# Experts with 4 KB weight rows, tokens fetched as rows by indirect DMA, results kept as rows in memory

## The chip, the cores and the metric

The kernel runs on one core of a Trainium2 chip. The metric is the device time of one execution in microseconds (us). Three runs of the kernel before gave 1471.57, 1472.33 and 1472.89 us, a median of 1472.33. The engines are PE (TensorE, matrix products), ACT (ScalarE), DVE (VectorE), POOL (GpSimd) and SP (SyncE, which only issues the weight loads here). PE reads its operands from SBUF, the on-chip memory, and writes to PSUM, which has eight banks of 512 float32 columns; ACT and DVE read PSUM, POOL does not.

## The reference

Two layers act on 256 tokens of 1024 values. Layer 0 is a mixer (sparse attention beside a gated delta rule) and a dense SwiGLU; layer 1 is a pooling mixer and a mixture of experts. Only the last stage is touched:

```python
def moe_ffn(x, router_w, wg, wu, wd):
    logits = jnp.einsum('bsd,de->bse', x, router_w).astype(F32)
    probs = jax.nn.softmax(logits, -1)
    top_p, top_i = lax.top_k(probs, TOP_K)                # 2 of 8
    top_p = top_p / jnp.sum(top_p, -1, keepdims=True)
    gate = jnp.sum(jax.nn.one_hot(top_i, N_EXPERTS) * top_p[..., None], axis=-2)
    y = jnp.zeros(x.shape, F32)
    for e in range(N_EXPERTS):
        y = y + gate[..., e:e + 1] * swiglu(x, wg[e], wu[e], wd[e])
    return y
```

`swiglu(x, wg, wu, wd)` is `(silu(x wg) * (x wu)) wd`, with wg and wu of 1024 x 3584 and wd of 3584 x 1024, all float32. A layer norm of `alpha * x + y` follows, which is the kernel's output. The eight experts hold 352 MB of weights, all of which are read.

## The kernel before, in words

The experts are worked through one after the other. Each computes on a buffer of C = 96 token slots; where an expert has more tokens than that, a loop behind a branch at the end does the rest (`tc.If(most > C)`).

Weights arrive in loads of 1 MB (`wchunk`, line 151) that SP issues into 16 staging buffers (`stg`), used in turn. Each load is worked on in two halves of 128 x 1024. ACT rounds a half into a high part `wh` (line 180), DVE subtracts it from the original for the low part `wl` (line 183), and there are four buffers of each. PE multiplies three times for each product (`mm3`, lines 187 to 189): low activations by high weights, high by low, high by high. For the gate weights of the first block of expert 0 the subtraction is given to POOL (`first`), and the rounding waits for `after`, a column of ones made from the routing.

An expert's 3584 hidden columns are seven blocks of 512. `up_block(b)` loads two 1 MB pieces of gate weights and two of up weights, each as rows of 512 columns (2 KB), accumulates them in two PSUM banks (`accg`, `accu`), then `swiglu_block` (lines 866 to 874) applies silu on ACT, multiplies on DVE, turns the 96 x 512 result with four PE transposes (`htp`) and splits it into a high and a low part in `hbc`. `down_block(b)` multiplies that with two 1 MB pieces of down weights (rows of 4 KB) into two banks `dacc`, held for the whole expert. Block b's `down_block` is written behind block b + 1's `up_block`.

Tokens enter and leave by PE. `gather(e)` (line 1059) makes a one-hot matrix `oh` of tokens by slots on DVE, multiplies the 256 x 1024 tokens `xt` by it on PE (16 matmuls of float32, which the trace shows as 32, into `gb`), splits the result into `ehl` (high and low), and transposes `oh` (`ohT`, copied to `ot`). It is issued ahead, in the previous expert's last block. At an expert's end `dacc` is split, PE multiplies it by `ot` (8 matmuls `scat`, lines 1125 and 1126), and DVE adds the result, times the gate, to `yt` (line 1128), which starts as `alpha * xt` (line 1150).

The order within each engine is set at build time by a scheduler that works with priorities and its own estimate of times; `wchunk`'s two halves have a high priority, and blocks under `urgent` a higher one.

Of the kernel before, what the change touches and what calls it, by code (L numbers as in the profile page):

```python
# [12 lines left out]
F32 = mybir.dt.float32  # L13
F32R = mybir.dt.float32r
# [94 lines left out]
def hybrid_kernel(ctx, tc, consts, bands, x, ev_w_in, ev_cmp_pe_k, ev_cmp_w_k, ev_cmp_pe_v, ev_cmp_w_v, ev_conv_w,  # L109
# [737 lines left out]
    def m_tile(i, name, dt=F32):  # L847
        return mp.tile([P, STG], dt, name=name, tag="m%d" % i)
# [196 lines left out]
    eh, el = (r3(ehl[:, o:o + KT * C], C) for o in (0, HALF))  # L1045
    hbc = r3(m_tile(2, "hbc", F32R), 512)
    turn = [0]

    def hpair():
        turn[0] ^= 2  # L1050
        return (hbc[:, turn[0] + i] for i in range(2))

    def bc(ap):
        return ap[:, :, None].to_broadcast(e3)
# [1 line left out]
    iota = cst("iota")  # L1056


    def gather(e):
        oh = late.tile([P, TT, C], F32, name="oh", tag="oh")  # L1060
        for t in range(TT):
            V.tensor_scalar(oh[:, t, :], iota[:, :C], rank[:, t, e:e + 1], sel[:, t, e:e + 1], op0=OP.is_equal, op1=OP.mult)
        for half in range(2):
# [7 lines left out]
        tp = bank("ohT", ps_tp)  # L1071
        for t in range(TT):
            T.transpose(tp[:C, t * P:(t + 1) * P], oh[:, t, :], ident)
        ot = late.tile([P, S], F32R, name="ot", tag="ot", bufs=2)[:C]
        A.copy(out=ot, in_=tp[:C, :S])
        return ot

    def expert(wg, wu, wd, gathered, gcol, ahead=None, after=None):
        ot = gathered
        dacc = [bank("dacc")[:C] for _ in range(2)]  # L1080
        nblk = DFE // 512
        def up_block(b):
            f0 = b * 512
            ac = {}
            for nm, wsrc in (("g", wg), ("u", wu)):
                ac[nm] = bank("acc" + nm)[:C]
# [6 lines left out]
            hb, hc = (r3(v[:, :4 * C], C) for v in hpair())  # L1093
            swiglu_block(ac["g"], ac["u"], 512, hb, hc, C)
            return hb, hc

        def down_block(b, hb, hc):
            last = b == nblk - 1
            loads = [wd[:, 4 * b + 2 * c:4 * b + 2 * c + 2, :] for c in range(2)]
            wcs = [wchunk([(src, D)], D) for src in loads] if last else None  # L1100
            for nbs in ([0], [1]) if last else ([0, 1],):
                for c in range(2):
                    wc = wcs[c] if last else wchunk([(loads[c], D)], D)
                    for k in range(2):
                        for nb in nbs:
                            mm3(dacc[nb], hb[:, 2 * c + k, :], hc[:, 2 * c + k, :], wc[k][0][:, nb * 512:(nb + 1) * 512],
                                wc[k][1][:, nb * 512:(nb + 1) * 512], b == 0 and c == 0 and k == 0,
                                last and c == 1 and k == 1)

        prev = up_block(0)  # L1110
        nxt = None
        for b in range(1, nblk):
            cur = up_block(b)
            if b == nblk - 1 and ahead is not None:
                nxt = gather(ahead)
            down_block(b - 1, *prev)
            prev = cur
        down_block(nblk - 1, *prev)
        ys_ = []
# [10 lines left out]
        return nxt  # L1130

    eg, eu, ed = od_exp_wg[0], od_exp_wu[0], od_exp_wd[0]
    sums = late.tile([P, TT, 2], F32, name="sums")
    with urgent(FIRST):
        got = gather(0)
# [10 lines left out]
    V.tensor_tensor(out=gate, in0=gate, in1=bc(m0), op=OP.mult)  # L1146
    nmax = late.tile([P, 1], I32, name="nmax")
    V.tensor_reduce(out=nmax, in_=rk[:, 16:24], axis=AX.X, op=OP.max)
    for t in range(TT):
        A.activation(yt[:, t, :], xt[:, t, :], AF.Copy, scale=late1[:, 1:2])  # L1150
    for e in range(NE):
        got = expert(krows(eg[e]), krows(eu[e]), krows(ed[e]), got, gate[:, :, e], e + 1 if e + 1 < NE else None,
                     after if e == 0 else None)

    g4, b4 = load_pair(od_ln2_g[0], od_ln2_b[0], stage_c[0].tile([P, STG], F32, name="g4b4", tag="stg"))

# [2 lines left out]
    with tc.If(most > C):  # L1159
        ring.clear()  # L1160
        stages[:] = [(stage_a, 4)]
        with tc.For_i(0, ROUNDS - 1, 1):
            V.tensor_scalar(rank, rank, -float(C), None, op0=OP.add)
            with tc.For_i(0, NE, 1) as i:
                def sub(w):
                    return w[bass.ds(i, 1)].rearrange("o (k p) n -> p (o k) n", p=P)

                expert(sub(eg), sub(eu), sub(ed), gather(0), gate[:, :, 0])
# [46 lines left out]
```

## Time and profile before

| | |
|---|---|
| median of three runs | 1472.33 us |
| profiled execution | 1473.03 us |
| its span, first to last instruction | 1471.2 us |
| PE busy | 1427.8 us (97%) |
| DVE busy | 1184.3 us (80%) |
| ACT busy | 976.8 us (66%) |
| DMA, mean over the span | 283 GB/s |

The experts begin with the first gather at 450.3 us and end about 15 us before the span does. The page's "busy" of PE overlaps from one matmul to the next: a 512-column matmul is listed with 0.39 us, yet the next starts about 0.23 us later. So starts are compared below, not durations. Each row of the timeline gives start, length, engine, line, operation, what it writes and reads, and how many instructions are merged; brackets give idle time before it and who ended it.

### The profile page before, as it was taken

What the parts mean: (1) busy time and instruction counts of PE and PEld (TensorE: products, weight loads), DVE (VectorE), ACT (ScalarE), POOL (GpSimd) and SP (SyncE); (2) the same over time, 40 slices, a digit from 0 to 9 for tenths busy, and PEclk for the clock granted to TensorE, in tenths of its full rate; (3) what the DMA queues carried; (4) which work ended last, traced back from release to release, by engine and by line L of the source; (5) the groups of instructions that cost most, each with busy time, mean ns of one, the idle gap of its engine ahead of it and who ended that gap; (6) DMA issues with size and microseconds to landing.
All of it is one profiled execution on the core that took longest, in us unless ns stands there. A gap on an engine that the chain in (4) does not pass through costs nothing. (4 is left out here: it accounts for less than half of the span.)

```text
span 1471.2 us, 18925 instructions
## 1 busy us (share of the span) xinstructions
PE 1427.8 (97%) x7006; PEld 1061.2 (72%) x7006; DVE 1184.3 (80%) x1524; ACT 976.8 (66%) x1216; POOL 20.0 (1%) x12
## 2 busy tenths in 40 slices
PE   8999988999998999999999999999999999999995
PEld 7898567888786777777777777777777777777663
DVE  6876655555567998999899899899989989989886
ACT  5745543444427777777777777777777777777773
POOL 0000020000002000000000000000000000000000
PEclk9999998999998999999999999999999999999998
DMA  8432039554864998999899899999989989999921
GB/s 294 141 104 101 1 101 330 183 189 158 307 223 166 378 373 323 362 371 370 314 372 373 312 372 371 343 344 371 370 312 375 372 321 364 367 347 335 353 113 60
DMA packets 188628, 416.89 MB, mean 283 GB/s; under 512 B 14104, under 2 KB 24816, under 8 KB 188528
## 3 DMA queue, kind: packets, MB, share of 16 engines
q1 hardware_dynamic: 188528, 415.61, 78.6%
q8 instruction: 57, 0.93, 0.3%
q14 instruction: 43, 0.35, 0.1%
HBM read 414.53 MB, written 1.05 MB: 282 GB/s over the span
## 5 line engine op out<-in xcount | busy, mean ns | idle before, releaser
L183 DVE TENSOR_TENSOR wl<-stg,wh 128x1024 fp32r<-128x1024 f32 (+1 forms) x765 | 914.3, 1221 | 181.9 <-ACT wh L180 174.5
L180 ACT CAST wh<-stg 128x1024 fp32r<-128x1024 f32 (+1 forms) x769 | 799.3, 1049 | 289.0 <-PE accg L189 81.7
L187 PE MATMUL accg<-wh,ehl 128*96 128x512 f32 x448 | 178.8, 399 | 1.9 <-DVE ehl L183 1.5
L188 PE MATMUL accg<-wl,ehl 128*96 128x512 f32 x448 | 177.3, 396 | 1.1 <-DVE wl L183 1.1
L188 PE MATMUL dacc<-wl,hbc 128*96 128x512 f32 x448 | 176.9, 395 | 0.0
L188 PE MATMUL accu<-wl,ehl 128*96 128x512 f32 x448 | 176.6, 394 | 0.2 <-DVE wl L183 0.2
L189 PE MATMUL accu<-wh,ehl 128*96 128x512 f32 x448 | 176.6, 394 | 0.0
L189 PE MATMUL accg<-wh,ehl 128*96 128x512 f32 x448 | 176.6, 394 | 0.0
L187 PE MATMUL accu<-wh,ehl 128*96 128x512 f32 x448 | 176.3, 394 | 0.0
L189 PE MATMUL dacc<-wh,hbc 128*96 128x512 f32 x448 | 175.9, 393 | 0.0
L187 PE MATMUL dacc<-wh,hbc 128*96 128x512 f32 x448 | 143.7, 393 | 0.0
L188 PEld LDWEIGHTS accu<-wl,ehl 128*96 128x96 f32 x448 | 72.1, 161 | 33.6 <-DVE wl L183 2.6
L188 PEld LDWEIGHTS accg<-wl,ehl 128*96 128x96 f32 x448 | 72.2, 161 | 33.5 <-DVE wl L183 2.9
L187 PEld LDWEIGHTS accg<-wh,ehl 128*96 128x96 f32 x448 | 72.3, 161 | 31.8 <-DVE ehl L183 2.0
L189 PEld LDWEIGHTS accg<-wh,ehl 128*96 128x96 f32 x448 | 72.6, 162 | 30.8
L189 PEld LDWEIGHTS accu<-wh,ehl 128*96 128x96 f32 x448 | 72.3, 161 | 31.2
L187 PEld LDWEIGHTS accu<-wh,ehl 128*96 128x96 f32 x448 | 72.1, 161 | 31.3
L187 PEld LDWEIGHTS dacc<-wh,hbc 128*96 128x96 f32 x448 | 72.2, 161 | 30.3
L189 PEld LDWEIGHTS dacc<-wh,hbc 128*96 128x96 f32 x448 | 72.2, 161 | 29.5
L188 PEld LDWEIGHTS dacc<-wl,hbc 128*96 128x96 f32 x448 | 72.4, 162 | 27.0 <-DVE wl L183 0.5
L869 ACT ACTIVATE hs<-accg 96x512 f32<-96x512 f32 (+2 forms) x68 | 39.5, 581 | 18.2 <-PE accg L189 17.2
L870 DVE TENSOR_TENSOR hs<-hs,accu 96x512 f32<-96x512 f32 (+2 forms) x68 | 45.6, 671 | 3.9 <-PE accu L189 3.9
(371 smaller groups left out, 1715.1 us busy)
## 6 DMA issues: line engine op xcount, KB each, us to landing
stg<-in_od_exp_wg_dram SPq DMA_DIRECT2D x112, 1024.0 KB, 5.3
stg<-in_od_exp_wu_dram SPq DMA_DIRECT2D x112, 1024.0 KB, 5.7
stg<-in_od_exp_wd_dram SPq DMA_DIRECT2D x112, 1024.0 KB, 5.6
stg<-in_ev_w_in_dram SPq DMA_DIRECT2D x13, 1024.0 KB, 6.4
stg<-in_ev_ffn_wg_dram SPq DMA_DIRECT2D x11, 1024.0 KB, 7.6
stg<-in_ev_ffn_wu_dram SPq DMA_DIRECT2D x11, 1024.0 KB, 5.6
stg<-in_ev_ffn_wd_dram SPq DMA_DIRECT2D x11, 1024.0 KB, 4.8
stg<-in_ev_w_out_dram SPq DMA_DIRECT2D x4, 1024.0 KB, 4.9
```

The source lines that it names most:

```text
L180: A.copy(out=hi, in_=src)
L183: (eng or V).tensor_tensor(out=lo, in0=src, in1=hi.bitcast(F32), op=OP.subtract)
L187: T.matmul(acc, lhsT=ll, rhs=rh, start=first, stop=False)
L188: T.matmul(acc, lhsT=lh, rhs=rl, start=False, stop=False)
L189: T.matmul(acc, lhsT=lh, rhs=rh, start=False, stop=last)
L869: A.activation(hs, gacc[:n, :width], AF.Silu)
L870: V.tensor_tensor(out=hs, in0=hs, in1=uacc[:n, :width], op=OP.mult)
```

## The change

Five things are altered together.

- Gate and up weights are taken in blocks of 1024 columns (three of 1024 and one of 512 for each expert), so that a 1 MB load is rows of 4 KB and holds two of the eight row groups (`nk = STG // width`). Each block has two banks each for `accg` and `accu`. `dacc` is allocated at the first `down_block`, and the hidden blocks have four pairs of buffers (`pairs`). The four loads of expert 0's first gate block take the POOL path (two before).
- The tokens are written to memory (`xd`) by POOL's DMA queue once. From expert 1 on, `fetch` computes the 96 token numbers (a bf16 one-hot, two matmuls of one column) and POOL gathers the rows with one indirect DMA into `rowbuf`; `turned` transposes them with eight PE transposes. Expert 0 keeps `gather`.
- Experts 0 to 6 copy `dacc` to `rowbuf` on ACT and store it as rows of `yd` (`store`). Expert 7 keeps the multiplication with `ot`.
- Near the routing DVE works out, for each token, the two rows of `yd` and their gates (`rowno`, `two`, `gates`).
- `collect`, in expert 7 behind its second block, starts `yt` from `alpha * xt`, gathers 256 rows twice by four indirect DMAs into two staging buffers, and adds them with four DVE operations of 128 x 1024.

```diff
-    b8 = late.tile([KT, P], F32, name="b8")
+    b8 = late.tile([P, TT * C], F32, name="b8", tag="oh")[:KT, :P]
...
-    yt = r3(m_tile(0, "yt"), D)
+    rowbuf = r3(m_tile(0, "rowbuf"), D)
...
+    def slots(e, dt=F32):
+        oh = late.tile([P, TT * C], F32, name="oh", tag="oh")
+        oh = r3(oh if dt is F32 else oh[:, :C].bitcast(dt), C)
+        for t in range(TT):
+            V.tensor_scalar(oh[:, t, :], iota[:, :C], rank[:, t, e:e + 1], sel[:, t, e:e + 1], op0=OP.is_equal, op1=OP.mult)
+        return oh
...
+    def fetch(e):
+        ohb = slots(e, BF16)
+        ix = bank("ix", ps_tp)[:C, 0:1]
+        for t in range(TT):
+            T.matmul(ix, lhsT=ohb[:, t, :], rhs=number[:, t:t + 1], start=t == 0, stop=t == TT - 1)
+        idx = late.tile([P, 1], I32, name="idx", tag="idx")[:C]
+        V.tensor_copy(idx, ix)
+        nc.gpsimd.indirect_dma_start(out=rowbuf[:C, 0], out_offset=None, in_=xd,
+                                     in_offset=bass.IndirectOffsetOnAxis(ap=idx, axis=0))
+
+    def turned():
+        for half in range(2):
+            gb = bank("gb", ps_tp)
+            for j in range(4):
+                k = 4 * half + j
+                T.transpose(gb[:, j * C:(j + 1) * C], rowbuf[:C, 0, k * P:(k + 1) * P], cst("ident", C)[:, :C])
+            split(eh[:, 4 * half:4 * half + 4, :], el[:, 4 * half:4 * half + 4, :], r3(gb[:, :4 * C], C))
...
+    BLOCKS = [(f0, min(1024, DFE - f0)) for f0 in range(0, DFE, 1024)]
...
-                for c in range(2):
-                    wc = wchunk([(wsrc[:, 4 * c:4 * c + 4, f0:f0 + 512], 512)], 512, *first)
-                    for k in range(4):
-                        kk_ = 4 * c + k
-                        mm3(ac[nm], eh[:, kk_, :], el[:, kk_, :], *wc[k], kk_ == 0, kk_ == KT - 1)
+                for c in range(KT // nk):
+                    wc = wchunk([(wsrc[:, nk * c:nk * c + nk, f0:f0 + width], width)], width, *first)
+                    for k in range(nk):
+                        kk_ = nk * c + k
+                        for i, acc in enumerate(ac[nm]):
+                            hs_ = slice(i * 512, (i + 1) * 512)
+                            mm3(acc, eh[:, kk_, :], el[:, kk_, :], wc[k][0][:, hs_], wc[k][1][:, hs_],
+                                kk_ == 0, kk_ == KT - 1)
...
+    def store(e, dacc):
         for nb in range(2):
-            yh_, yl_ = (v[:C] for v in hpair())
+            A.copy(out=rowbuf[:C, 1, nb * 512:(nb + 1) * 512], in_=dacc[nb])
+        nc.gpsimd.dma_start(out=yd[1 + e * C:1 + (e + 1) * C, :], in_=rowbuf[:C, 1])
...
+    for t in range(TT):
+        nc.gpsimd.dma_start(out=xdv[:, t, :], in_=xt[:, t, :])
...
+    V.tensor_scalar(rowno, rank, float(C), None, op0=OP.is_lt)
+    V.tensor_tensor(out=rowno, in0=rowno, in1=sel, op=OP.mult)
...
+    for e in range(NE - 1):
+        V.scalar_tensor_tensor(rowno[:, :, e], rank[:, :, e], float(1 + e * C), rowno[:, :, e], op0=OP.add, op1=OP.mult)
...
+    def collect():
+        ybuf = r3(m_tile(0, "yt"), D)
+        for t in range(TT):
+            A.activation(ybuf[:, t, :], xt[:, t, :], AF.Copy, scale=ALPHA)
+        for i in range(2):
+            rows = r3(stage_tile(), D)
+            for t in range(TT):
+                nc.gpsimd.indirect_dma_start(out=rows[:, t, :], out_offset=None, in_=yd,
+                                             in_offset=bass.IndirectOffsetOnAxis(ap=twoi[:, i, t:t + 1], axis=0))
+            for t in range(TT):
+                V.scalar_tensor_tensor(ybuf[:, t, :], rows[:, t, :], gates[:, i, t:t + 1], ybuf[:, t, :],
+                                       op0=OP.mult, op1=OP.add)
...
+    for e in range(NE):
+        end = e == NE - 1
+        dacc = expert(krows(eg[e]), krows(eu[e]), krows(ed[e]), None if end else e + 1, after if e == 0 else None,
+                      collect if end else None)
+        if not end:
+            store(e, dacc)
+        if e == NE - 2:
+            lot = places(slots(NE - 1))
```

Three places show how the engines' orders move. The first is PE at the end of an expert, where the tokens of the next one are brought in; before, in the last block of expert 0 (`dacc` is the running down product):

```order
L873 MATMUL htp<-keep,hs 128x96 x4
L1068 MATMUL gb<-oh,xt 128x96 x8
L188 MATMUL dacc<-wl,hbc 96x512
L189 MATMUL dacc<-wh,hbc 96x512
L188 MATMUL dacc<-wl,hbc 96x512
L189 MATMUL dacc<-wh,hbc 96x512
L1068 MATMUL gb<-oh,xt 128x96 x8
L187 MATMUL dacc<-wh,hbc 96x512
```

The same place on PE after the change:

```order
L873 MATMUL htp<-keep,hs 128x96 x4
L1110 MATMUL gb<-keep,rowbuf 128x96 x4
L188 MATMUL dacc<-wl,hbc 96x512
L189 MATMUL dacc<-wh,hbc 96x512
L188 MATMUL dacc<-wl,hbc 96x512
L189 MATMUL dacc<-wh,hbc 96x512
```

Two runs of eight gather matmuls (sixteen rows each in the trace) have become two runs of four transposes; the second run stands twenty rows further on.

The second place is DVE between the routing and the first expert. `ehl` is what expert 0's first matmul reads. Before:

```order
L1062 TENSOR_SCALAR oh<-keep,route 128x96 x2
L183 TENSOR_TENSOR ehl<-gb,ehl 128x384
L1062 TENSOR_SCALAR oh<-keep,route 128x96 x2
L183 TENSOR_TENSOR ehl<-gb,ehl 128x384
L1140 TENSOR_SCALAR late_4000<-ehl 128x1
L1141 TENSOR_SCALAR late_4000<-late_4000 128x1
L183 TENSOR_TENSOR wl<-stg,wh 128x1024
```

After the change, on DVE at the same place:

```order
L1071 TENSOR_SCALAR oh<-keep,route 128x96 x2
L1221 TENSOR_SCALAR pick<-route 128x16
L1222 TENSOR_TENSOR pick<-pick,route 128x16
L1223 MEMSET pick 128x2
L1225 SCALAR_TENSOR_TENSOR pick<-route,pick 128x2 x7
L1226 TENSOR_REDUCE two<-pick 128x2
L1227 TENSOR_REDUCE two<-pick 128x2
L1233 TENSOR_TENSOR pick<-pick,two 128x16
L1228 TENSOR_TENSOR two<-two 128x2
L1230 CAST twoi<-two 128x4
L183 TENSOR_TENSOR ehl<-gb,ehl 128x384
```

Fifteen small operations now stand ahead of the split that expert 0 waits for.

The third place is POOL's queue, where the change differs from before as follows (the subtractions of line 183 stood in one row of eight before, four for the dense SwiGLU and four for expert 0):

```order
 L183 ISA
+L183 TENSOR_TENSOR wl<-stg,wh 128x1024 x4
+L1218 DMA yd<-rowbuf 16x1x64
+L1194 DMA xd<-xt 128x1024 x2
 L183 TENSOR_TENSOR wl<-stg,wh 128x1024 x8
```

Expert 0 now has eight subtractions on POOL, and three stores to memory are issued ahead of them; 7 fetches, 7 stores and 4 gathers of rows follow.

## Rows read from the trace of the kernel before

**Rows 1.** The page's first part: busy us of an engine (share) xinstructions.

```profile
PE 1427.8 (97%) x7006; PEld 1061.2 (72%) x7006; DVE 1184.3 (80%) x1524; ACT 976.8 (66%) x1216; POOL 20.0 (1%) x12
```

**Rows 2.** Stretches: length; busy us (x count) of PE, PEld, DVE, ACT, POOL; PEclk, DMA share, GB/s.

```profile
456.40:480.00 23.60, 21.47 (x95) 14.34 (x94) 20.53 (x24) 20.63 (x24) 3.95 (x2) 1.00 0.83 290
480.00:570.00 90.00, 90.00 (x404) 63.16 (x403) 82.18 (x76) 70.54 (x75) 0.00 (x0) 1.00 1.02 374
697.00:821.00 124.00, 124.00 (x572) 88.16 (x571) 112.31 (x112) 94.79 (x103) 0.00 (x0) 1.00 0.97 355
```

**Rows 3.** Waits: engine, tile and line, whom it waited for: us in total, times, longest.

```profile
DVE wl L183 <- ACT wh L180: 174.5, 317, 5.1
ACT wh L180 <- PE accg L189: 81.7, 169, 2.5
SPq L161 <- DVE wl L183: 1037.5, 353, 67.2
```

**Rows 4.** DMA issues: tile and source, count, size, median us from issue to landing.

```profile
stg<-in_od_exp_wg_dram SPq DMA_DIRECT2D x112, 1024.0 KB, 5.3
```

**Rows 5.** Timeline, PE: two block starts of expert 1, one block apart.

```profile
640.45 0.63 PE L187 MATMUL dacc<-wh,hbc 128*96 128x512 f32 x2
657.43 0.63 PE L187 MATMUL dacc<-wh,hbc 128*96 128x512 f32 x2
```

**Rows 6.** Timeline, PE: end of expert 0, and the same gather one expert later.

```profile
571.77 1.95 PE L1068 MATMUL gb<-oh,xt 128*128 128x96 f32 x16
573.51 0.45 PE L188 MATMUL dacc<-wl,hbc 128*96 128x512 f32 x1
...
577.88 0.38 PE L1073 MATMUL ohT<-keep,oh 128*96 128x128 f32 x2
578.02 0.47 PE L188 MATMUL dacc<-wl,hbc 128*96 128x512 f32 x1
...
586.43 0.39 PE L1125 MATMUL scat<-hbc,ot 96*128 96x512 f32 x1
...
587.36 0.40 PE L187 MATMUL accu<-wh,ehl 128*96 128x512 f32 x1
...
696.31 1.95 PE L1068 MATMUL gb<-oh,xt 128*128 128x96 f32 x16
```

**Rows 7.** Timeline, PE: four transposes and the matmuls behind them.

```profile
645.04 0.49 PE L873 MATMUL htp<-keep,hs 96*128 96x96 f32 x4
...
645.31 0.45 PE L187 MATMUL accg<-wh,ehl 128*96 128x512 f32 x1
...
645.60 0.39 PE L188 MATMUL dacc<-wl,hbc 128*96 128x512 f32 x1
```

**Rows 8.** Timeline: POOL, DVE and PE at the start of expert 0.

```profile
451.00 9.36 POOL L183 TENSOR_TENSOR wl<-stg,wh 128x1024 fp32r<-128x1024 f32 x4 [229.82 <-ACT wh L182]
454.96 0.56 DVE L183 TENSOR_TENSOR ehl<-gb,ehl 128x384 fp32r<-128x384 f32 x1 [4.58 <-ACT ehl L180]
456.42 0.48 PE L187 MATMUL accg<-wh,ehl 128*96 128x512 f32 x1
456.71 3.71 DVE L1062 TENSOR_SCALAR oh<-keep,route 128x96 f32<-128x96 f32 x2 [1.19 <-PE ohT L1073]
460.94 0.47 PE L187 MATMUL accg<-wh,ehl 128*96 128x512 f32 x1 [1.50 <-DVE ehl L183]
```

**Rows 9.** One line's instructions (xcount: ns min/median/max), here `oh`.

```profile
L1062 DVE TENSOR_SCALAR oh<-keep,route x16: 323/330/2405, 449.8 to 1201.2; 128x96 f32<-128x96 f32 x16
```

**Rows 10.** Timeline: POOL and DVE in the dense SwiGLU's start, and one DVE operation alone.

```profile
215.55 5.63 POOL L183 TENSOR_TENSOR wl<-stg,wh 128x1024 fp32r<-128x1024 f32 x2 [0.33 <-ACT wh L180]
215.76 3.21 DVE L225 SCALAR_TENSOR_TENSOR tmp<-xt,lnsm,stg 128x1024 f32<-128x1024 f32 x1
438.37 1.29 DVE L225 SCALAR_TENSOR_TENSOR tmp<-xt,lnsm,g3b 128x1024 f32<-128x1024 f32 x1
```

**Rows 11.** Timeline, DVE: three low parts in a row in the block of rows 5.

```profile
642.10 3.60 DVE L183 TENSOR_TENSOR wl<-stg,wh 128x1024 fp32r<-128x1024 f32 x3
```

More of the change, by code (lines that the diff above doesn't have):

```diff
@@ L1070, in gather @@
             split(eh[:, 4 * half:4 * half + 4, :], el[:, 4 * half:4 * half + 4, :], gb)
-        tp = bank("ohT", ps_tp)
+        return oh
+    def fetch(e):
+        ohb = slots(e, BF16)
+        ix = bank("ix", ps_tp)[:C, 0:1]
         for t in range(TT):
[L1073 to L1081, printed above, removed]
+            T.matmul(ix, lhsT=ohb[:, t, :], rhs=number[:, t:t + 1], start=t == 0, stop=t == TT - 1)
[3 more added lines that the diff above has]
+                                     in_offset=bass.IndirectOffsetOnAxis(ap=idx, axis=0))
@@ new lines, in turned, with expert @@
+    def turned():
[6 more added lines that the diff above has]
+    BLOCKS = [(f0, min(1024, DFE - f0)) for f0 in range(0, DFE, 1024)]
+    def expert(wg, wu, wd, ahead=None, after=None, during=None):
+        dacc = []
@@ L1100, in down_block @@
+            made = []
+            for ga, ua in zip(ac["g"], ac["u"]):
+                made.append(hpair())
+                swiglu_block(ga, ua, 512, *made[-1], C)
+            return made
+        def down_block(b, made):
+            if b == 0:
+                dacc.extend(bank("dacc")[:C] for _ in range(2))
+            last = b == len(BLOCKS) - 1
+            f0, width = BLOCKS[b][0] // P, BLOCKS[b][1] // P
+            loads = [wd[:, f0 + f:f0 + f + 2, :] for f in range(0, width, 2)]
             wcs = [wchunk([(src, D)], D) for src in loads] if last else None
@@ L1101, in down_block @@
             for nbs in ([0], [1]) if last else ([0, 1],):
-                for c in range(2):
-                    wc = wcs[c] if last else wchunk([(loads[c], D)], D)
+                for c, src in enumerate(loads):
+                    wc = wcs[c] if last else wchunk([(src, D)], D)
                     for k in range(2):
+                        hb, hc = made[(2 * c + k) // 4]
+                        f = (2 * c + k) % 4
                         for nb in nbs:
-                            mm3(dacc[nb], hb[:, 2 * c + k, :], hc[:, 2 * c + k, :], wc[k][0][:, nb * 512:(nb + 1) * 512],
-                                wc[k][1][:, nb * 512:(nb + 1) * 512], b == 0 and c == 0 and k == 0,
-                                last and c == 1 and k == 1)
+                            hs_ = slice(nb * 512, (nb + 1) * 512)
+                            mm3(dacc[nb], hb[:, f, :], hc[:, f, :], wc[k][0][:, hs_], wc[k][1][:, hs_],
+                                b == 0 and c == 0 and k == 0, last and c == len(loads) - 1 and k == 1)
@@ L1110, in expert @@
         prev = up_block(0)
-        nxt = None
-        for b in range(1, nblk):
+        if ahead is not None:
+            fetch(ahead)
+        for b in range(1, len(BLOCKS)):
             cur = up_block(b)
-            if b == nblk - 1 and ahead is not None:
-                nxt = gather(ahead)
-            down_block(b - 1, *prev)
+            if b == 1 and during is not None:
+                during()
+            if b == len(BLOCKS) - 1 and ahead is not None:
+                turned()
+            down_block(b - 1, prev)
@@ L1117, in expert, with scatter @@
             prev = cur
-        down_block(nblk - 1, *prev)
-        ys_ = []
+        down_block(len(BLOCKS) - 1, prev)
+        return dacc
+    def store(e, dacc):
         for nb in range(2):
-            yh_, yl_ = (v[:C] for v in hpair())
+            A.copy(out=rowbuf[:C, 1, nb * 512:(nb + 1) * 512], in_=dacc[nb])
+        nc.gpsimd.dma_start(out=yd[1 + e * C:1 + (e + 1) * C, :], in_=rowbuf[:C, 1])
+    def scatter(dacc, ot, gcol):
+        for nb in range(2):
+            yh_, yl_ = (hbc[:C, (2 * nb + i) * 512:(2 * nb + i + 1) * 512] for i in range(2))
@@ new lines, in hybrid_kernel @@
+    V.tensor_copy(twoi, two)
+    gates = late.tile([P, 2, TT], F32, name="gates")
+    for i in range(2):
+        V.tensor_tensor(out=hit, in0=rowno, in1=bc(two[:, i]), op=OP.is_equal)
+        V.tensor_tensor(out=hit, in0=hit, in1=gate, op=OP.mult)
+        V.tensor_reduce(out=gates[:, i], in_=hit, axis=AX.X, op=OP.add)
+    kept = {}
+    def collect():
+        ybuf = r3(m_tile(0, "yt"), D)
+        for t in range(TT):
+            A.activation(ybuf[:, t, :], xt[:, t, :], AF.Copy, scale=ALPHA)
+        for i in range(2):
+            rows = r3(stage_tile(), D)
[5 more added lines that the diff above has]
+                                       op0=OP.mult, op1=OP.add)
+        kept["yt"] = ybuf
@@ L1155, in hybrid_kernel @@
+    for e in range(NE):
+        end = e == NE - 1
[5 more added lines that the diff above has]
+            lot = places(slots(NE - 1))
+    yt = kept["yt"]
+    scatter(dacc, lot, gate[:, :, NE - 1])
     g4, b4 = load_pair(od_ln2_g[0], od_ln2_b[0], stage_c[0].tile([P, STG], F32, name="g4b4", tag="stg"))
@@ L1166, in sub @@
                     return w[bass.ds(i, 1)].rearrange("o (k p) n -> p (o k) n", p=P)
-                expert(sub(eg), sub(eu), sub(ed), gather(0), gate[:, :, 0])
+                ot = places(gather(0))
+                scatter(expert(sub(eg), sub(eu), sub(ed)), ot, gate[:, :, 0])
                 sh = late.tile([P, 3, TT, NE], F32, name="sh", tag="sh")
```

56 lines of the change are left out of this document (37 added, 19 removed).

## The prediction

> **What bounds the kernel now.** I read the page's first part [rows 1], then the stretches of the expert stage [rows 2], the waits [rows 3] and, last, single rows of the timeline. In rows 1 the reader is to see that PE is busy for 1427.8 us, 97%; an average over the span, so it needs a stage. In rows 2 the 124.0 us from 697 to 821 are full of PE (124.0), while DVE has 112.31 and ACT 94.79. DMA is no looser: its share is 0.97 there and 1.02 from 480 to 570, at 374 GB/s. So PE and the loads are both near their end, and the waits must tell which is late. They do [rows 3]: SP waits 1037.5 us, in 353 pieces, for DVE to give back staging buffers, DVE waits 174.5 us for ACT's rounding, ACT waits for PE to free a `wh`. Each waits for the one nearer PE, and no row names a load as what an engine waited for. The loads are ahead by up to the 16 staging buffers. A block of expert 1 lasts 657.43 - 640.45 = 16.98 us [rows 5] and uses six loads, 2.83 us each; 16 of them are 45 us, and a load needs 5.3 us [rows 4]. PE sets the time, and an instruction taken from it between two blocks shortens the kernel.
>
> **What leaves PE at an expert's end.** From one gather to the same one an expert later are 696.31 - 571.77 = 124.54 us [rows 6]. Seven blocks are 7 x 16.98 = 118.86. The difference, 5.68 us, is the traffic of tokens through PE. Counted from the other side: the gather is two runs, each 573.51 - 571.77 = 1.74; the `ohT` pair 578.02 - 577.88 = 0.14; the eight scatter matmuls 586.43 to 587.36 are 0.93 for the first four and as much again for the other four, 1.86 in all. Together 5.48, and 0.2 us of refilling between kinds of matmul. I take 5.68.
>
> **What comes to PE.** Eight transposes in two runs. A run of four takes 645.31 - 645.04 = 0.27 us [rows 7], and the next matmul starts about 0.06 later than its pace; two runs are 0.66. The two one-column matmuls of `fetch` I put at 0.15 us, as much as the two `ohT` transposes (0.14), with 0 and 0.34 as ends. Net 5.68 - 0.66 - 0.15 = 4.87 us for each of seven boundaries (expert 0 still gathers and expert 7 still multiplies by `ot`): -34.1 us, and a period of 119.67 us. The row gather has the time: it is written behind the first block and needed in the last, over 75 us later at 16.98 us for 512 columns. The store needs the next use of the same half of `rowbuf` to be an expert later, and it is.
>
> **The start of expert 0.** Before, PE runs 21.47 of the 23.60 us from 456.4 to 480 [rows 2], a loss of 2.13, mostly because DVE stood. POOL works at four subtractions from 451.00 to 460.36, 2.34 us each [rows 8], and DVE's two `oh` operations beside them need 3.71 us together, one of them 2405 ns where 330 is usual [rows 9]: each ends when a subtraction of POOL does. The same is in rows 10: DVE's 3.21 us beside two of POOL's, 1.29 us alone. But the `ehl` split, with one input in PSUM, took 0.56 beside them [rows 8]. So a DVE operation whose inputs all lie in SBUF stands until POOL's current one ends, and gets one turn before POOL's next. After the change fifteen small operations stand ahead of that split, of which some ten have SBUF inputs alone and are of such a kind; three or four pass before POOL starts. POOL runs its first four in one row (until the `wl` buffers are full), so the rest pass at the three gaps and behind the fourth, and the split comes near 461 in place of 454.96, the first matmul near 461.6 in place of 456.42: +5.2 us. Then POOL has four more subtractions, 9.36 us, against DVE's gate operations and its first `wl`; each of these turns costs up to 2.34, and I take +4.3. That is 9.5 lost where 2.13 were before: +7, with +1.5 as the low end (small operations are not held: the fifteen then end before the gather does) and +10 as the high one.
>
> The Trainium skill (SBUF — State Buffer, "Who interferes with whom") says that the pair of ports that DVE and GpSimd share is an exclusive lock, held for a whole instruction, so that the one that comes second stands until its end. Rows 8 to 10 agree for 128x96 and 128x1024; no row shows a 128x2 beside POOL. By that rule the start costs the +7 taken; if only large operations stood it would be +1.5.
>
> **Collect in expert 7.** Four DVE operations of 128x1024, 1.29 us each alone [rows 10], are 5.2 us in which no `wl` is made. A block uses up twelve halves, one in 16.98 / 12 = 1.415 us, and DVE makes one in 3.60 / 3 = 1.20 [rows 11], so it wins back 0.215 us at each. I let it do so over the twelve halves around `collect`, 2.6 us, and take +2.5 for the rest, with ends 0 and 5.2 (all or nothing won back). The gathered rows hold two of 16 staging buffers; the loads' lead of 45 us covers that. The two ACT operations that began `yt` at the start move here and lie beside PE.
>
> **POOL's row transfers.** Seven fetches, seven stores and four gathers are 18 that the trace of before doesn't show in this stage. If they never touch DVE, 0; if each holds it as POOL's subtraction held the operation in rows 10 (3.21 - 1.29 = 1.9), 18 x 1.9 = 34. DVE's waits for ACT [rows 3] show slack of 174.5 us, so I take the low end's side, +1.
>
> **4 KB rows.** 0, since no engine waits for a load. What covers this is thin: an expert's 44.04 MB and the 0.79 MB of fetched and stored rows in 119.67 us ask for 374.6 GB/s, and rows 2 show 374 over 90 us. A shortfall of 5 us in every expert would be met by the 45 us of lead for seven experts and then show. The gate and up matmuls now take two banks in turn, as `dacc` does. Its 20 from 640.45 to 645.04 [rows 5, 7] come at 0.2295 us; the block's other 48 at (16.98 - 24 x 0.2295 - 0.33) / 48 = 0.232. If the banks' order makes that difference, 0.0026 x 48 x 56 blocks = 7 us go; a copy behind an accumulator could do as much, so I take 0, with -7 as the low end.
>
> The Trainium skill (DMA: Bandwidth & Descriptors, "Specifications") gives a limit of about 358 GB/s of HBM for one core; 44.83 MB would take 125.2 us an expert, and nothing would be gained. Rows 2 show 374 GB/s for 90 us with only this core at work, so the measurement decides and the rule gets a small chance.
>
> **Sum.** -34.1 + 7 + 2.5 + 1 + 0 = -23.6 us on the profiled 1473.03: 1449.4. The median of three runs lies 0.7 lower, so about 1449.
>
> **The rivals.**
> - The start is cheap and the new order of matmuls gives its 7 us: -34.1 + 1.5 + 2.5 - 7 = -37, 1435. For it: the fifteen are tiny, and `dacc` does run faster. Against it: rows 9.
> - DVE is late inside the long blocks. A block of 1024 has two products and two splits in a row on DVE where before one came at a time; that is two operations more ahead of the next `wl`, at DVE's mean of 112.31 / 112 = 1.00 us [rows 2]. If 0.6 us of these 2 show on PE at each of 24 long blocks, 14 us go: 1463. For it: DVE has 112.31 of 124.0 already, and of 119.67 now. Against it: four `wl` buffers are 4 x 1.415 = 5.7 us of PE's work, and DVE's waits show slack.
> - Slower: POOL's row transfers hold DVE for a subtraction's length. Each would cost the `oh` row's excess, 2.405 - 0.33 = 2.08 us [rows 9], and 18 of them 37.4 in place of my 1: about 1486. It decides from 24 / 18 = 1.3 us each. For it: DVE's margin in the stage is 10%, and POOL and DVE do exclude each other. Against it: a transfer's issue isn't a read of 128x1024, and DVE has (124.0 - 112.31) / 84 = 0.14 us to spare at each of an expert's 84 halves.
> - The loads set the pace: at the 355 GB/s of rows 2 from 697 to 821, an expert's 44.83 MB need 126.3 us, and the lead of 45 us is eaten at 6.6 an expert. Against it: 355 there is what PE asked for, not a limit. About 1472, no change.
>
> **How the numbers follow.** Forecast, 1441 to 1457: 0.55 (the ends of the start, of collect and half of the transfers' bound). Cheap start: 0.15. Late DVE: 0.19. Loads: 0.03. POOL holding DVE: 0.08. The range from 1434 to 1464 takes in the first three but for their tails. A change of 0.2%, 2.9 us, is about the least that a measurement of this kernel can tell. The first three are faster by more than that, 0.89; the loads' case is the same, 0.03; POOL's slower, 0.08.
>
> **What would show it.** The profile after should have 0.27 us runs of transposes where the gather stood, no `scat` before expert 7, and a period near 119.7 us. At the start the first `accg` near 461, POOL with eight subtractions of about 2.34 us, and 7 to 10 us of idle PE named for DVE. In expert 7 some 2.5 us of PE idle beside the four additions of `collect`. DVE's `wl` should keep its length beside the row transfers; if it grows, the slower rival is at work. I am wrong if PE waits for `wl` in blocks between, if a wait names `stg` or `rowbuf`, or if the first matmul starts before 458.

## The result, and the profile after

The changed kernel took 1454.22 us (median of four runs, 1452.95 to 1455.19) where the kernel before took 1472.54: a ratio of 0.9876, with a 95% interval of 0.9859 to 0.9893. That is 18.3 us less; 23.6 were forecast. The profiled execution took 1455.19 us, of which the span is 1453.4.

Two tables of starts tell where the time went. First rows of the kernel before that were not shown yet, from PE's timeline: the gather of expert 0, the first `accg` of experts 1 and 7, and the last `dacc`.

```profile
450.29 6.16 PE L1068 MATMUL gb<-oh,xt 128*128 128x96 f32 x32 [0.72 <-DVE oh L1062]
...
582.03 0.40 PE L187 MATMUL accg<-wh,ehl 128*96 128x512 f32 x1
...
1329.90 0.40 PE L187 MATMUL accg<-wh,ehl 128*96 128x512 f32 x1
...
1452.43 0.39 PE L189 MATMUL dacc<-wh,hbc 128*96 128x512 f32 x1
```

The same places of the changed kernel, and the two runs of transposes that stand where the gather stood [rows 6].

```profile
451.55 5.96 PE L1089 MATMUL gb<-oh,xt 128*128 128x96 f32 x32 [0.72 <-DVE oh L1071]
462.25 0.74 PE L187 MATMUL accg<-wh,ehl 128*96 128x512 f32 x1 [4.75 <-DVE ehl L183]
...
477.81 0.74 PE L188 MATMUL accu<-wl,ehl 128*96 128x512 f32 x1 [3.22 <-DVE wl L183]
...
577.64 0.49 PE L1110 MATMUL gb<-keep,rowbuf 96*128 96x96 f32 x4
577.92 0.45 PE L188 MATMUL dacc<-wl,hbc 128*96 128x512 f32 x1
...
583.02 0.49 PE L1110 MATMUL gb<-keep,rowbuf 96*128 96x96 f32 x4
583.30 0.45 PE L187 MATMUL dacc<-wh,ehl 128*96 128x512 f32 x1
...
590.26 0.40 PE L187 MATMUL accg<-wh,ehl 128*96 128x512 f32 x1
...
1306.79 0.39 PE L187 MATMUL accg<-wh,ehl 128*96 128x512 f32 x1
...
1434.12 0.39 PE L189 MATMUL dacc<-wh,hbc 128*96 128x512 f32 x1
```

A run of four transposes takes 0.28 us. By stage, in the profiled executions:

| stage | before | after | difference |
|---|---|---|---|
| up to expert 0's gather | 450.29 | 451.55 | +1.26 |
| gather to the first `accg` | 6.13 | 10.70 | +4.57 |
| expert 0, first `accg` to the next expert's | 125.61 | 128.01 | +2.40 |
| experts 1 to 6 | 747.87 | 716.53 | -31.34 |
| expert 7, first `accg` to last `dacc` | 122.53 | 127.33 | +4.80 |
| to the end of the span | 18.7 | 19.3 | +0.5 |

An expert of the middle lasts 716.53 / 6 = 119.42 us, 5.22 less than 747.87 / 6 = 124.65. Expert 0 saves only its part of that (5.22 less the scatter that it never had, 1.86), and expert 7 the scatter of expert 6, 1.86; so the seven boundaries give 36.5 us (the wide blocks' part of it included), the start took 1.26 + 4.57 + 2.40 + 3.36 = 11.6 of it back, and expert 7, where `collect` stands, 4.80 + 1.86 = 6.7.

The windows view of the changed kernel for the start and for the stretch of [rows 2]: length; busy us (count) of PE, PEld, DVE, ACT, POOL; granted clock, DMA share, GB/s.

```profile
462.25:481.00 18.75, 14.81 (x48) 9.58 (x49) 12.35 (x21) 9.06 (x9) 9.47 (x4) 0.77 0.38 121
481.00:496.00 15.00, 15.00 (x62) 10.25 (x61) 11.15 (x11) 12.11 (x13) 0.00 (x0) 0.92 0.91 329
476.60:483.40 6.80, 5.59 (x13) 3.72 (x14) 4.21 (x5) 2.09 (x2) 0.00 (x0) 0.50 0.51 161
...
697.00:821.00 124.00, 124.00 (x565) 87.54 (x564) 113.75 (x109) 99.01 (x108) 1.48 (x2) 1.00 1.00 377
```

In the middle PE is as full as before and the DMA moves 377 GB/s. At the start PE stands for 3.9 us behind its first `accg`, and the granted clock is 0.77, then 0.92, a mixture of its two levels (1.2 and 2.4 GHz), where before it was 1.00 [rows 2]. The row from 476.60 to 483.40, in which PE ends a wait of 3.22 us, is at the lower level throughout (0.50).

**What the start shows.** DVE and POOL of the changed kernel, timeline (start, length, engine, line).

```profile
441.68 0.91 DVE L1217 MEMSET rowbuf<- 1x1024 f32 x1 [0.15 <-issue]
...
452.05 2.75 DVE L1225 SCALAR_TENSOR_TENSOR pick<-route,pick 128x2 f32<-128x2 f32 x6
454.84 0.17 DVE L1226 TENSOR_REDUCE two<-pick 128x2 f32<-128x16 f32 x1
...
455.04 2.11 DVE L1233 TENSOR_TENSOR pick<-pick,two 128x16 f32<-128x16 f32 x1
457.08 2.36 DVE L1228 TENSOR_TENSOR two<-two 128x2 f32<-128x2 f32 x1
459.47 2.27 DVE L1230 CAST twoi<-two 128x4 int32<-128x4 f32 x1
461.66 0.54 DVE L183 TENSOR_TENSOR ehl<-gb,ehl 128x384 fp32r<-128x384 f32 x1
...
452.27 9.45 POOL L183 TENSOR_TENSOR wl<-stg,wh 128x1024 fp32r<-128x1024 f32 x4 [2.54 <-ACT wh L182]
```

Operations on 2 to 16 values of a lane last 2.1 to 2.4 us beside POOL's four subtractions, one for each of the last three, and the split that expert 0 needs comes at 461.66. The reduction between them takes 0.17. The zeroing of the 4 KB row, which the prediction didn't price, runs on one partition for 0.91 us in the middle of the layer norm's chain.

**What expert 7 shows.** PE, ACT and SP of the changed kernel around `collect`.

```profile
1358.39 1.17 PE L187 MATMUL dacc<-wh,ehl 128*96 128x512 f32 x2 [5.05 <-ACT wh L180]
...
1357.30 1.99 ACT L180 CAST wh<-stg 128x1024 fp32r<-128x1024 f32 x2 [3.44 <-DMA stg<-in_od_exp_wd_dram]
...
1296.45 8.93 SPq L161 DMA_DIRECT2D stg<-in_od_exp_wu_dram  x4
1324.30 9.44 SPq L161 DMA_DIRECT2D stg<-in_od_exp_wg_dram  x4
1336.56 8.64 SPq L161 DMA_DIRECT2D stg<-in_od_exp_wu_dram  x4
1347.11 17.78 SPq L161 DMA_DIRECT2D stg<-in_od_exp_wd_dram  x8
```

PE stands 5.05 us, not for DVE's additions but for ACT, and ACT for a load of down weights. The first row of SP is the up weights of expert 7's second block. Then SP issued nothing from 1305 to 1324, then the third block's gate and up weights, and the first down weights, for which PE stood from 1353, only from 1347. One expert earlier, at the same place in the queue:

```profile
1177.09 8.11 SPq L161 DMA_DIRECT2D stg<-in_od_exp_wu_dram  x4
1187.11 9.13 SPq L161 DMA_DIRECT2D stg<-in_od_exp_wd_dram  x4
1198.14 9.10 SPq L161 DMA_DIRECT2D stg<-in_od_exp_wg_dram  x4
```

There four down loads follow the second block's up loads; in expert 7 the third block's eight loads stand ahead of them. The stall has a second price. Behind it the granted clock was at its lower level (the row's 0.50):

```profile
1358.39:1364.00 5.61, 5.51 (x12) 3.28 (x13) 5.41 (x5) 3.93 (x4) 0.00 (x0) 0.50 1.03 410
```

Matmuls came 0.43 us apart there (1362.33, 1362.75, 1363.18) in place of 0.23; over the twelve that is some 2.4 us. The stall and this are about 7.4 us, more than the 6.7 that expert 7 lost as a whole.

### The profile page after: what moved, and what is told of

It is laid out like the page before. It is cut to its first block, busy times and chain, and to the rows that moved or that the text cites. A ratio compares the mean times of both kernels' runs of the same rounds, so it can differ in the third digit from the quotient of the medians.

```text
span 1453.4 us, 18472 instructions
## 1 busy us (share of the span) xinstructions
PE 1395.5 (96%) x6782; PEld 1032.0 (71%) x6782; DVE 1163.9 (80%) x1488; ACT 968.3 (67%) x1209; POOL 69.1 (5%) x37
## 5 line engine op out<-in xcount | busy, mean ns | idle before, releaser
L183 DVE TENSOR_TENSOR wl<-stg,wh 128x1024 fp32r<-128x1024 f32 (+1 forms) x761 | 899.4, 1220 | 178.3 <-ACT wh L180 168.9
L180 ACT CAST wh<-stg 128x1024 fp32r<-128x1024 f32 (+1 forms) x765 | 786.7, 1050 | 257.2 <-PE accu L189 81.9
L189 PE MATMUL accg<-wh,ehl 128*96 128x512 f32 x448 | 177.0, 395 | 0.0
L189 PE MATMUL accu<-wh,ehl 128*96 128x512 f32 x448 | 176.4, 394 | 0.0
L187 PE MATMUL accg<-wh,ehl 128*96 128x512 f32 x448 | 146.7, 396 | 4.7 <-DVE ehl L183 4.7
L187 PE MATMUL accu<-wh,ehl 128*96 128x512 f32 x448 | 146.0, 394 | 0.7 <-ACT wh L180 0.7
L188 PE MATMUL dacc<-wl,hbc 128*96 128x512 f32 x336 | 134.0, 399 | 0.1
L189 PE MATMUL dacc<-wh,hbc 128*96 128x512 f32 x336 | 133.0, 396 | 0.0
L188 PEld LDWEIGHTS dacc<-wl,hbc 128*96 128x96 f32 x336 | 54.6, 162 | 24.1 <-DVE wl L183 2.4
L187 PE MATMUL dacc<-wh,hbc 128*96 128x512 f32 x224 | 71.6, 394 | 0.0
L189 PEld LDWEIGHTS dacc<-wh,hbc 128*96 128x96 f32 x336 | 54.7, 163 | 21.4 <-issue 0.3
L187 PEld LDWEIGHTS dacc<-wh,hbc 128*96 128x96 f32 x224 | 35.8, 161 | 15.1
```

The lines of the kernel that those rows point to most:

```text
L180: A.copy(out=hi, in_=src)
L183: (eng or V).tensor_tensor(out=lo, in0=src, in1=hi.bitcast(F32), op=OP.subtract)
L187: T.matmul(acc, lhsT=ll, rhs=rh, start=first, stop=False)
L188: T.matmul(acc, lhsT=lh, rhs=rl, start=False, stop=False)
L189: T.matmul(acc, lhsT=lh, rhs=rh, start=False, stop=last)
```

## The experiments

All have the changed kernel as their base unless they say otherwise. The kernel before ran beside each (1472.5 us).

**The rows' numbers, later.** `row_numbers()` holds lines 1221 to 1235 and its first operand depends on expert 1's tokens.

```diff
+        V.tensor_scalar(hold, el[:, KT - 1, 0:1].bitcast(F32), 0.0, float(C), op0=OP.mult, op1=OP.add)
+        V.tensor_scalar(rowno, rank, hold[:, 0:1], None, op0=OP.is_lt)
...
+        if e == 0:
+            row_numbers()
```

> The changed kernel with one thing moved: the operations that work out each token's two rows and their gates wait for expert 1's tokens instead of standing ahead of the ehl split of expert 0. Theory: they are what the split stood behind, each small operation getting one turn between two of POOL's subtractions. Then the split ends about 2 us after the gather as in the kernel before, the first matmul of expert 0 comes 6 us after the gather's first in place of 10.7, and the idle PE of 3.2 us at 474 us shrinks with the later turns: 6 to 9 us less, 1445 to 1448 us. Rival: the eight subtractions of POOL are themselves the delay, whatever stands on DVE; then the first matmul comes early but the time is lost again in the first block, 0 to 2 us less.

1446.09 us, 8.1 less, as the theory had it. The first `accg` came 5.5 us after the gather. Expert 0 still lasted 126.65 us: the operations left beside POOL were held in their turn. Not all of the gain is the start's: in the profiled execution expert 7, which the edit doesn't touch, was 2.1 us shorter, with a stall of 2.9 us in place of 5.05.

**Collect last.**

```diff
-            if b == 1 and during is not None:
+            if b == 3 and during is not None:
```

> The changed kernel with collect called in expert 7's last block instead of its second. All its work stays. Theory: the 5.3 us of idle PE at 1353 us come from the order of loads on SP's queue: the four loads of the first down block stand behind eight of the third gate and up block, because collect's two staging buffers were taken just ahead of them; with collect last the loads go out in the order of use, the stall and the slower matmuls behind it are gone: 5 to 8 us less, 1446 to 1449. Rival: DVE's four additions and the two ACT scalings are what PE waits for; then the wait only moves to the last block and the time stays within 2 us of 1454.

1451.26 us, 3.0 less: between the two. The loads kept their order and none was waited for, but three of the additions ran in a row (3.67 us) ahead of the product that the transposes need, and PE stood 2.79 us for it.

**No additions.**

```diff
-            for t in range(TT):
-                V.scalar_tensor_tensor(ybuf[:, t, :], rows[:, t, :], gates[:, i, t:t + 1], ybuf[:, t, :],
-                                       op0=OP.mult, op1=OP.add)
```

> The changed kernel without collect's four additions of 128x1024 on DVE (the rows are fetched and not added, so experts 0 to 6 are missing from the output). The queue of loads keeps the changed kernel's order. Theory: the stall at 1353 us stays in full, since it is a load that is late, and the additions had room: 0 to 2 us less, 1452 to 1454. Rival, the prediction's own step: the additions are the cost, 5 to 8 us less.

1453.60 us, 0.6 less, which is within the noise. The stall stays without the additions, 4.3 us long (2.9 to 5.5 in the runs with wide blocks that leave `collect` at its place); they are not its cause.

**Blocks of 512.**

```diff
-    BLOCKS = [(f0, min(1024, DFE - f0)) for f0 in range(0, DFE, 1024)]
+    BLOCKS = [(f0, min(512, DFE - f0)) for f0 in range(0, DFE, 512)]
```

> The changed kernel with gate and up blocks of 512 columns again, so rows of 2 KB and one bank at a time; fetch, store and collect as changed. Theory: token traffic is what gained, and the 4 KB rows and the banks in turn give only about 0.35 us for each expert (a period of 119.42 us where 119.67 was worked out from the blocks of 512): 0 to 4 us more, 1454 to 1458, with a period near 119.7 us. Rival: the rows of 4 KB keep the loads ahead; with 2 KB the loads fall behind inside the experts, PE waits for staging buffers' landings there, and the period grows by over 1 us: 1462 or more.

1472.71 us, a ratio of 1.0002 (0.9992 to 1.0011) to the kernel before: the whole gain is gone. The theory missed; the time lies where the rival put it, but not for the rival's reason. The experts had periods of 120.7 us (experts 1 and 2), then 121.7 and 123.1, so they still gained 15 us on the kernel before; expert 7 lost 12.6, with a stall of 10 us for a load like the one above. No load was waited for before expert 7. What PE waited for was DVE, at the block ends: in the first experts once at each boundary, and from expert 3 on within the experts. The second run of transposes at the end of expert 1, then ACT and PE of expert 4:

```profile
698.14 0.55 PE L1110 MATMUL gb<-keep,rowbuf 96*128 96x96 f32 x4 [0.84 <-DVE ehl L183]
...
1040.14 1.05 ACT L180 CAST wh<-stg 128x1024 fp32r<-128x1024 f32 x1 [0.35 <-PE accu L189]
1043.72 0.48 ACT L180 CAST hbc<-htp 128x384 fp32r<-128x384 f32 x1 [2.53 <-PE htp L873]
1044.10 4.86 ACT L180 CAST wh<-stg 128x1024 fp32r<-128x1024 f32 x5
...
1045.81 0.39 PE L187 MATMUL accg<-wh,ehl 128*96 128x512 f32 x1
1046.47 0.48 PE L188 MATMUL accg<-wl,ehl 128*96 128x512 f32 x1 [0.27 <-DVE wl L183]
```

In expert 4 ACT stands 2.53 us with the cast of the transposes at the head of its queue and five roundings behind it; PE then starts 0.66 us after its last matmul in place of 0.23. Four or five such places in an expert are 2 us.

**Rows of 2 KB in blocks of 1024.**

```diff
-                    wc = wchunk([(wsrc[:, nk * c:nk * c + nk, f0:f0 + width], width)], width, *first)
+                    wc = wchunk([(wsrc[:, nk * c:nk * c + nk, f0 + o:f0 + o + 512], 512) for o in range(0, width, 512)], width, *first)
```

> The changed kernel with its blocks of 1024 columns, but each 1 MB piece of gate and up weights brought in by two loads of 512 columns (rows of 2 KB), so that only the length of the rows is as before. It is to say which half of the 1024-column blocks the 18 us come from by which the blocks of 512 were slower. Theory: not the rows: with blocks of 512 no engine waited for a landing before expert 7, PE waited for DVE's low parts right behind block ends, where ACT's queue stands 2.5 us before the cast of the transposes; blocks of 1024 have half as many ends. Then this stays within 4 us of the changed kernel: 1452 to 1458, period 119.2 to 120. Rival: the rows of 2 KB are dearer for the loads, which ask for 374 GB/s: period over 121 us and PE waiting for landings, 1465 or more.

1452.99 us, with periods of 118.9 to 119.5: the length of the rows does nothing that the noise would let show. So it is the width of the blocks that does.

**Wide blocks alone.** The kernel before with the changed `BLOCKS`, `up_block`, `down_block` and `pairs`.

```diff
-                turned()
+                nxt = gather(ahead)
...
-        if not end:
-            store(e, dacc)
...
+        scatter(dacc, got, gate[:, :, e])
+        if nxt is not None:
+            got = places(nxt)
```

> The kernel before with the gate and up blocks of 1024 columns alone (rows of 4 KB, banks in turn, four pairs of hidden buffers, eight subtractions on POOL for the first block); tokens still go in and out through PE in every expert, and there is no collect. Theory: PE's traffic of tokens is what the change removed, so this keeps a period near 124 us (0.5 less from the pace of the matmuls); 1466 to 1474. Rival: as the blocks of 512 with rows in memory gained nothing, the wide blocks carry the gain by themselves: a period near 121 and 1450 to 1458.

1470.03 us (ratio 0.9983, 0.9974 to 0.9993): the theory. The period is 124.05 us, 0.5 less than before.

**No subtractions on POOL.**

```diff
-                first = (after, nc.gpsimd) if after is not None and nm == "g" and b == 0 else ()
+                first = (after, None) if after is not None and nm == "g" and b == 0 else ()
```

> The changed kernel with expert 0's first eight subtractions on DVE in place of POOL; the fifteen small operations stay where they are, ahead of the ehl split. Theory: it is POOL's subtractions beside DVE that made the start slow, by holding each small operation; without them the fifteen take 2 to 3 us and end before the gather does, the first matmul of expert 0 comes about 6 us after the gather's first (10.7 before), the idle 3.2 us at 474 us are gone though DVE has eight subtractions of 1.2 us more, and the slower clock behind the idle time too: 8 to 12 us less, 1442 to 1446. Rival: the number of DVE's operations is the cost; then DVE, with 9.6 us more, makes it slower: 1456 to 1462.

1442.40 us, 11.8 less, as the theory had it, though DVE does eight subtractions more. The same operations as above, and the stretch from this kernel's first `accg`:

```profile
452.03 0.44 DVE L1225 SCALAR_TENSOR_TENSOR pick<-route,pick 128x2 f32<-128x2 f32 x5
...
454.81 0.17 DVE L1233 TENSOR_TENSOR pick<-pick,two 128x16 f32<-128x16 f32 x1
454.89 0.15 DVE L1228 TENSOR_TENSOR two<-two 128x2 f32<-128x2 f32 x1
...
456.57 0.16 DVE L1230 CAST twoi<-two 128x4 int32<-128x4 f32 x1
```

```profile
457.06:481.00 23.94, 23.94 (x107) 16.80 (x107) 21.01 (x35) 21.05 (x23) 0.00 (x0) 1.00 0.82 309
```

2.11, 2.36 and 2.27 us have become 0.17, 0.15 and 0.16. PE is busy all the time, at the full clock, and expert 0 lasts 119.07 us, no longer than the others.

**All mended.** The last, the first and two more edits:

```diff
-            if b == 1 and during is not None:
+            if b == 2 and during is not None:
...
-    V.memset(rowbuf[:1, 1], 0.0)
+    nc.gpsimd.memset(rowbuf[:1, 1], 0.0)
```

> The changed kernel with four things mended: expert 0's subtractions on DVE, the row numbers and gates worked out behind expert 1's tokens, the zeroing of the 4 KB row on POOL in place of DVE, and collect in expert 7's third block, where the loads keep nearly the order of their use and the four additions stand apart from each other. Theory: the start gives 10 to 13 us, the zeroing 1, collect 5 to 7 of its 8: 1434 to 1440. If collect's stall only moves, as it did in part with collect in the last block, 1440 to 1445. Rival: the additions cost what they cost wherever they stand and POOL was no loss: 1448 or more.

1439.64 us, 14.6 less than the changed kernel and a ratio of 0.9779 (0.9763 to 0.9795) to the kernel before. It is within the theory's first range, at its upper end, but its parts are not as expected: the subtractions on DVE alone gave 11.8, so the other three mends gave 2.8 on top, where 6 to 8 were expected of the zeroing and `collect`. The loads are in order; what is left in expert 7 is a row of short waits, one for ACT and five for DVE, whose additions (L1254) now stand between low parts:

```profile
1374.46 0.70 PE L187 MATMUL dacc<-wh,hbc 128*96 128x512 f32 x2 [0.92 <-ACT wh L180]
1375.72 0.47 PE L188 MATMUL dacc<-wl,hbc 128*96 128x512 f32 x1 [0.56 <-DVE wl L183]
1378.05 0.47 PE L188 MATMUL dacc<-wl,hbc 128*96 128x512 f32 x1 [0.73 <-DVE wl L183]
1380.38 0.47 PE L188 MATMUL dacc<-wl,hbc 128*96 128x512 f32 x1 [0.70 <-DVE wl L183]
1384.31 0.47 PE L188 MATMUL dacc<-wl,hbc 128*96 128x512 f32 x1 [0.91 <-DVE wl L183]
1386.64 0.47 PE L188 MATMUL dacc<-wl,hbc 128*96 128x512 f32 x1 [0.73 <-DVE wl L183]
...
1375.58 1.28 DVE L1254 SCALAR_TENSOR_TENSOR yt<-stg,gates,yt 128x1024 f32<-128x1024 f32 x1
1376.77 1.22 DVE L183 TENSOR_TENSOR wl<-stg,wh 128x1024 fp32r<-128x1024 f32 x1
1377.91 1.28 DVE L1254 SCALAR_TENSOR_TENSOR yt<-stg,gates,yt 128x1024 f32<-128x1024 f32 x1
```

**Blocks of 512, mended.** The mends with `BLOCKS` of 512 and collect in the fifth block (`b == 4`).

> Blocks of 512 columns with rows fetched and stored, and with the mends of the kernel that has all four (expert 0's subtractions on DVE, row numbers late, zeroing on POOL, collect in a block where the loads keep their order). It divides the gain: the blocks of 512 gave nothing when only the width was put back. Theory: there the experts gained 15 us, and the start and collect took it back; mended, the gain of fetch and store shows: periods of 120.7 to 123.1 us as they were, no stall of 10 us in expert 7, 1452 to 1458. Rival: without the wide blocks no gain is to be had: 1466 or more.

1456.72 us (ratio 0.9896, 0.9880 to 0.9913): the theory. Fetch and store are worth 15.8 us without the wide blocks, once start and collect don't take it back, and in the mended kernels the wide blocks give 17.1 more on top, where they gave 2.5 by themselves.

**Twice the row transfers.**

```diff
+        nc.gpsimd.indirect_dma_start(out=rowbuf[:C, 0], out_offset=None, in_=xd,
+                                     in_offset=bass.IndirectOffsetOnAxis(ap=idx, axis=0))
...
+        nc.gpsimd.dma_start(out=yd[1 + e * C:1 + (e + 1) * C, :], in_=rowbuf[:C, 1])
```

> The changed kernel with each fetch and each store of rows issued twice (the second does the same again): 14 more transfers on POOL's queue. Theory: a transfer costs PE nothing, since it doesn't hold DVE and the loads have room: 1452 to 1457. Rival: each holds DVE as a subtraction of POOL does, 1.9 us, with DVE at 90%: some 14 to 27 us more, 1468 to 1481. Between them, if the 11 MB more are what tips the loads: 1458 to 1464, and PE waiting for landings.

1455.89 us, the theory: 14 transfers more cost 1.7 us, 0.12 each. The runs of the two kernels overlap (1455.04 to 1458.76 beside 1452.95 to 1455.19), so this is hardly clear of the noise. DVE's `wl` beside them, first of this kernel, then of the changed one, with the fetches of the latter (ns min/median/max):

```profile
L183 DVE TENSOR_TENSOR wl<-stg,wh x662: 1208/1219/1229, 480.1 to 1430.9; 128x1024 fp32r<-128x1024 f32 x166
```

```profile
L183 DVE TENSOR_TENSOR wl<-stg,wh x662: 1208/1220/1229, 480.9 to 1430.1; 128x1024 fp32r<-128x1024 f32 x166
...
L1102 POOL DMA_INDIRECT rowbuf<-xd,idx x7: 932/5546/5556, 505.9 to 1217.2; - x7
```

A fetch keeps POOL for up to 5.6 us, 5.5 in the median, and no `wl` is longer for it.

**Collect in two halves.** All mended, but `during(0)` and `during(1)` in blocks 2 and 3, a staging buffer and two additions each.

> The kernel with all four mends, but collect in two halves: one staging buffer of rows and two additions in expert 7's third block, the other in its fourth. Theory: the four additions of 1.29 us hurt because they come in a lump that outlasts the low parts in stock; in pairs, half of it is won back: 1435 to 1438 (1439.6 with the lump). Rival: DVE has no time to win back in this stage, the additions cost their 5 us in any place: 1439 to 1441.

1439.43 us: the rival. Spreading the additions wins nothing.

**All mended, no additions.** The same three lines left out as above.

> The kernel with all four mends without collect's four additions (the rows are fetched and not added, so experts 0 to 6 are missing from the output). The loads keep the order that they have with them. Theory: with the loads in order, the additions are what is left of collect's price: 4 to 6 us less than 1439.6, so 1434 to 1436. Rival: ACT's queue or the loads hold PE there anyway: 1438 to 1440, as in the changed kernel, where leaving them out gave 0.6.

1435.28 us, 4.4 less than with them: the theory. With the loads in order, the four additions cost most of their own 5.2 us.

## Why the prediction was right, and where it was off

The sign and the range held, and the mechanism is the one forecast: token traffic left PE, 5.22 us at each boundary where 4.87 were worked out. The terms of the sum against the profile:

| term | forecast | measured |
|---|---|---|
| seven boundaries | -34.1 | -36.5 |
| start of expert 0 | +7 | +11.6 |
| collect (all that expert 7 lost) | +2.5 | +6.7 |
| row transfers on POOL | +1 | 0.12 each by the doubled ones, an estimate of 2 for 18, and within the terms above |
| 4 KB rows | 0 | 0 within the noise |

The terms were off by -2.4, +4.6, +4.2 and -1, 5.4 us together, and the range was wide enough for that.

- **What bounds it.** PE is full from boundary to boundary in the changed kernel too, so what left it shortened the period. It held in full only with the wide blocks, which the prediction took for free: it worked out 119.67 us from blocks of 512, where the runs with 512 had 120.7 to 123.1. That the measured 119.42 lies so near is luck: the prediction left out what blocks of 512 lose and what wide blocks give, and the two nearly cancel. PE's gather had not been the only thing between the blocks; with it gone, PE's waits for DVE at block ends show. The order "two banks in turn" was put at 0 with -7 as its end. The run with wide blocks alone gives 0.5 us a period for all that comes with them; no run changed the order by itself.
- **The start** was right in its place and short in its size. The first `accg` came at 462.25 (461.6 forecast), and it was DVE's small operations between POOL's subtractions. Three of them took a turn each, while six of L1225 passed in one. By the Trainium skill (SBUF — State Buffer, "Who interferes with whom") a reduction never takes the shared ports; the 0.17 us of L1226 beside the 2.11 us of L1233 agree. Two things were missing. One is the zeroing, 0.91 us ahead of the routing; of the 1.26 us by which the gather came later it is not more than a part, since with the same zeroing other runs began the gather at 450.28 to 450.92. The other is the lower clock behind the idle time: of the 8.6 us by which expert 0 was longer than the others, 3.9 are PE's idle time, and the rest, some 4.5, goes with the clock (granted 0.77 and 0.92; with no such idle time it was 1.00 and expert 0 lasted 119.07).
- **Collect** is the step that failed, and its measured price lies outside the bounds given (0 to 5.2). The prediction saw "DVE operations in which no `wl` is made" and let DVE win back half. In the changed kernel the price was a load that came late, 5.05 us, and the lower clock behind it, some 2.4: leaving the additions out gave 0.6 us. One of the prediction's own signs of being wrong, a wait that names `stg`, came up here. "The loads' lead of 45 us covers that" looked at how many buffers collect holds, and not at the order in which the loads behind it are issued. With the loads in order the additions do cost 4.4, near the upper bound: DVE wins little back.
- **The 4 KB rows** as such are 0 within the noise, shown by the rows of 2 KB. The Trainium skill's limit of about 358 GB/s (DMA: Bandwidth & Descriptors, "Specifications") did not bind: the changed kernel moved 377 GB/s for 124 us, where the kernel before asked for 355 [rows 2].
- **The rivals.** POOL's row transfers did not hold DVE. The late DVE in long blocks did not come about, but in short ones it did. The loads did not set the pace in the middle; their order did so once, in expert 7. A cheap start can be had, by another edit.

What stays open: in blocks of 512, why the scheduler puts the cast of the transposes ahead of the roundings in some experts and not in others (the kernel before has the same wait of 2.5 us only at the end of expert 6 and in expert 7, six times). No run changed that order by itself, so its price there is read from the trace and not shown. So it is open, too, how much of the 17.1 us that the wide blocks give beside the rows comes from having fewer block ends, and how much from what else changes with the width.

## What to carry to other kernels

When work leaves the bounding engine, look at what the other engines did in its shade: the gain of 5 us a boundary was only there in full when the blocks were wide too, and the wide blocks gave 2.5 us by themselves and 17.1 beside the rows. A buffer taken out of a ring in the middle of a stream must be checked in the order of the load queue, not only by how many buffers are left. A helper engine is no help where its operations hold those of the engine that it is to relieve: the kernel was faster by 11.8 us when DVE did all the work of expert 0 itself.

## What the runs showed of the hardware

- DVE operations on 128x2, 128x4 and 128x16 beside a row of POOL's subtractions of 128x1024 lasted 2.1 to 2.4 us, as long as one of these, and 0.15 to 0.17 without them. A reduction of 128x16 beside them lasted 0.17. That the small size plays no part was only argued before.
- In the 19 us behind 4.75 us of idle PE (with 3.9 us more of it among them) the granted clock was 0.77. Where it was 0.50, with 3.22 us of idle PE just before, matmuls came 0.43 us apart (479.62, 480.05, 480.48) in place of 0.23; behind 5.05 us of idle PE in expert 7 it was 0.50 again, for 5.6 us.
- An indirect fetch of 96 rows of 4 KB kept POOL for 0.9 to 5.6 us, 5.5 in the median, and landed 7.8 to 13.2 us after its issue; seven fetches and seven stores more cost the kernel 1.7 us, hardly more than its noise.
- One core moved 377 GB/s over 124 us, and the kernel whose gate and up loads had rows of 2 KB took no longer than that with rows of 4 KB (1452.99 and 1454.22 us).
